# A two-layer streaming encoder on one core: the merge of its instruction strands keeps the strand chosen last until another is 0.04 of its own length behind

## The chip, the cores and the metric

The kernel runs on one core of one Trainium2 chip. The metric is the device time of one execution in microseconds (us). The kernel before was executed three times for timing and once under the profiler. The engines are named as in the profile: PE is the matrix engine (PEld its weight load), DVE the vector engine, ACT the scalar engine, POOL the general engine, SP the engine that only starts transfers.

## What is computed

The input x has 512 tokens of width 1024 in float32, and there is a memory of 256 tokens. Layer 0 mixes its tokens by a recurrence over 12 heads of 64 (with attention of 4 more heads into the memory beside it), layer 1 by chunked attention over 12 heads (with the same memory attention). Each layer ends in a gated feed-forward part with a convolution of width 3. Cut to what matters here:

```python
def wkv7_scan(r, w, k, v, a, b):                  # layer 0, one step per token
    def step(state, inp):
        r_t, w_t, k_t, v_t, a_t, b_t = inp
        sa = einsum('bhvk,bhk->bhv', state, a_t)
        state = state * w_t + sa * b_t + v_t * k_t     # outer products, 64x64 a head
        return state, einsum('bhvk,bhk->bhv', state, r_t)
...
for layer in range(2):
    h = rms_norm(x, ln1[layer])
    p = h @ w_in[layer]
    if layer == 0:
        mix = rwkv7_time_mix(h, p[..., :3 * 768], ...)   # scan, norm per head, gate g
    else:
        mix = chunk_attention(q, k_pad, v_pad, bias)     # own chunk and 8 before
    mo = memory_attention(q_mem, mem_n, w_mem_kv[layer])
    x = x + concatenate([mix, mo]) @ w_out[layer]
    x = x + conv_glu(rms_norm(x, ln2[layer]), ...)
return rms_norm(x, ln_f)
```

## The kernel before

**Data and products.** Activations lie with features on the 128 partitions and the 512 tokens along the free axis. A float32 product is made of three products of rounded halves: high by high (L221), low by high (L222) and high by low (L225). A projection to 128 features is 24 such matmuls of 128x512 over 8 slices of the width. In the text they are called wide matmuls. Their weights come by DMA into `wraw`; ACT rounds the high half `whi` (L175), and DVE (L183) or ACT (L180) makes the low half `wlo`.

**The recurrence.** Heads go in six pairs, each in three parts, which are Python generators:

- `prepare(i)` (L1085) makes r, k, v and the decay of pair i with three projections (72 wide matmuls), normalises k over each head, mixes each projection with its shifted self (the results `krv` and `v`, L1121), makes the scores within each chunk of 64 tokens (L1169), copies them (ACT, L1174) and starts a triangular solve on DVE. The normalisation takes sums over heads, for pairs 2 and 3 in a wide form (`head_wide`: Square on ACT L1061, split L238, sums on PE L1065 and L1066), else in a narrow one (`head_rsqrt`: sums on PE L1041).
- `front(i)` (L1249) makes the parts of pair i that need no solve or only its first half: L1259 with its mask on DVE (L1262), row sums L1283 and L1285, a copy `Rq` on ACT (L1266), L1317 with the copy `Y` (L1323), and L1334 with four small copies `Tt` (L1339).
- `back(i)` (L1359) finishes pair i: L1369 and L1377, L1383 with its copy `Tt` (L1387), two halves of L1393 (copies L1394, L1396), two halves of L1404 (DVE L1405, L1406), L1412, then eight chunks in a row of the state (L1426 on PE, L1427 on DVE, L1431 on PE). The result is copied to `yc` (ACT L1435), the gate's weights are rounded (`g2h`, ACT L1442), yc is squared (L1441, or L1061 where `head_wide` is used, for pairs 1 and 2), its sums over heads are taken (PE L1041, or L1065) and the gate is multiplied (PE L201 to L203).

All of these but the wide matmuls have tiles of 64 rows or fewer on PE, except the sums over heads.

**The attention of layer 1** goes over the same pairs of heads. A row block (L1745, L1746) makes scores for 128 queries; DVE adds the bias and takes the maximum (L1750), ACT takes the exponential (L1752), DVE the reciprocal of the sum (L1753) and the product with it (L1754). Three row blocks later (`LAG = 3`) PE transposes the block (L1760) and ACT copies it (L1762). The values (L1774) follow at the end of a pair.

**What sets the order.** The engines each run their instructions in the order in which the program lists them, with semaphores between engines. That order is made by `weave` (L87). It is given several generators, here called strands, each with a length. A strand issues some instructions of all engines and then yields the time that its PE work is held to cost, which is added to its `done`; it may also yield a time for which it must not be called, or a condition. Of the strands that may be called, `weave` calls the one with the smallest share of its length done:

```python
e = min(ready, key=lambda x: x[2] / x[1])     # L99: done / length
```

Behind it a scheduler of the framework moves instructions within each engine's list where their inputs come late by its own costs, with the order of the program as priority. `weave` is called four times:

- L1530: the end of `prepare(0)` with the low-rank projections and the memory's keys and values;
- L1538, once for each stage 0 to 4: `back(stage - 1)`, `front(stage)` and `prepare(stage + 1)`, with the lengths 13.7, 5.8 and 18.7 us;
- L1566: `back(4)`, then `front(5)` and `back(5)`, the memory attention, and a part of the output projection;
- L1840: the attention of layer 1 (a length of 50.2 us by the program's own costs) with the projections of its queries, keys and values and a part of the output projection (84.4 us).

The dense strands yield after every two wide matmuls (0.43 us in the program's costs), the small parts after 0.15 to 2.3 us. The feed-forward parts are not woven.

**Buffers.** The PSUM banks are 8: two for wide matmuls; in layer 0 four for small products and two for long sums, in the attention six for small products. Weights have three `whi`, three `wlo` and two `wraw`.

Of the kernel before, what the change touches and what calls it, by code (L numbers as in the profile page):

```python
# [83 lines left out]
    return c  # L84


def weave(gens, tc=None):  # L87

    live = [[g[0], float(g[1]), 0.0, 0.0, g[2] if len(g) > 2 else 0, None] for g in gens]
    now = 0.0
    while live:
        free = [e for e in live if e[5] is None or e[5]()]
        ready = [e for e in free if e[3] <= now]
        if not ready:
            now = min(e[3] for e in free)
            continue
        e = min(ready, key=lambda x: x[2] / x[1])  # L99
        e[5] = None  # L100
        try:
            with tc.high_priority(e[4]) if e[4] else ExitStack():
                y = next(e[0])
        except StopIteration:
            live.remove(e)
            continue
        if callable(y):
            e[5] = y
            continue
        cost, wait = y if isinstance(y, tuple) else (y, 0)  # L110
        now += cost
        e[2] += cost
        e[3] = now + wait
# [3 lines left out]
def trunk_kernel(ctx, tc, A, out):  # L117
# [1410 lines left out]
    for d_ in d2s:  # L1528
        nc.sync.dma_start(d_[:].rearrange("b m g u c i -> (b m g u) (c i)"), zero[:, 0:256])
    weave([(first, .981 * PREP_COST), (chain(lora_one(), mem_kv()), 16 * 648 + MEMKV_COST)])  # L1530
    act1 = hact
    pre = []
    lo_on[0] = 1
    for st_ in range(NPAIR - 1):
        gens = [(front(st_, Ts[st_], Ts[st_ + 1]), 1.069 * FRONT_COST), (prepare(st_ + 1, Ts[st_ + 1]), .971 * PREP_COST)]
        if st_ > 0:
            gens.insert(0, (back(st_ - 1, Ts[st_ - 1], dst_mix), 1.003 * BACK_COST))
        weave(gens, tc)  # L1538
# [21 lines left out]
    def ahead():  # L1560
# [3 lines left out]
    AHEAD = [0, 1, 2, 3, 4, 6, 7]  # L1564
    a_, b_ = NPAIR - 2, NPAIR - 1
    weave([(told(back(a_, Ts[a_], dst_mix), "back"), 1.5 * BACK_COST),  # L1566
           (chain(front(b_, Ts[b_]), later(6000), back(b_, Ts[b_], dst_mix, other_tiles, lambda: "back" in over)),
            1.5 * (FRONT_COST + BACK_COST)),
# [420 lines left out]
```

## Time and profile before

| | us |
|---|---|
| median of three runs | 1302.93 (1302.65 to 1303.38) |
| the profiled execution: its own time | 1301.85 |
| the profiled execution: span of the page | 1300.1 |
| PE busy in the span | 1278.6 |
| stages of the recurrence, all calls of L1538 | about 83 to 302 |
| last weave of layer 0 | about 302 to 350 |
| attention of layer 1 | about 735 to 924 |

The span runs from the first to the last instruction of the profile; 1.75 us of the profiled execution's own time lie around it. Starts in the profile are counted from the beginning of the span. In a timeline row the first number is the start, the second the duration, and a bracket at the end gives how long the engine stood idle ahead of it and what released it. In order listings a count behind a row (x8) joins neighbours of one form; a row on the 64x64 products holds two heads, so that the profile's count for the same work is twice as high.

### The profile page before, as it was taken

To read this page: it belongs to the slowest core of one execution; us is meant where nothing else is said; L and a number is where in the kernel's file an instruction comes from. 1 tells how busy PE (TensorE), PEld (TensorE's weight loads), DVE (VectorE), ACT (ScalarE), POOL (GpSimd) and SP (SyncE) were. 2 spreads that over 40 slices of the span, in tenths; PEclk is the share of its full clock that TensorE was granted. 3 is DMA by queue.
4 is the path that set the end of the run, shared out by engine and by line. 5 is a ranking of instruction groups with operands and counts; after the bars stand their busy time and mean duration, and the time that the engine had idled before them with its cause. 6 is when DMAs were issued, how large, how long until landed. Compare 5 with 4: busy or idle time off the path is not lost.

```text
span 1300.1 us, 26329 instructions
## 1 busy us (share of the span) xinstructions
PE 1278.6 (98%) x10420; PEld 1100.9 (85%) x10420; DVE 1041.8 (80%) x1956; ACT 836.5 (64%) x1380; POOL 137.6 (11%) x164
## 2 busy tenths in 40 slices
PE   9999999999999999999999999999999999999997
PEld 7887777777789999999888878787799999998886
DVE  7967767775589999999876876658889999998684
ACT  6666767756566666767554676657757666665562
POOL 1000000000001112110220000000011122111200
PEclk9999999999999999999999999999999999999999
DMA  6365434452236777886984332223437878879951
GB/s 202 110 177 116 112 69 106 95 113 69 82 114 148 182 175 193 189 183 176 270 179 122 123 90 85 81 95 115 130 80 183 183 173 197 186 159 285 214 141 65
DMA packets 92988, 187.42 MB, mean 144 GB/s; under 512 B 21824, under 2 KB 30144, under 8 KB 92864
## 3 DMA queue, kind: packets, MB, share of 16 engines
q1 hardware_dynamic: 68592, 129.14, 31.1%
q0 software_dynamic: 24272, 56.59, 25.0%
q8 instruction: 82, 1.34, 0.4%
q14 instruction: 42, 0.34, 0.1%
HBM read 169.48 MB, written 6.29 MB: 135 GB/s over the span
## 4 chain that ended last, share of the span: by engine, by line
PE 83%; DVE 7%; ACT 6%; issue 1%; DMA 1%; SPq 0%; ACTq 0%; DVEq 0%
PE psf L414 21%; PE psf L416 11%; PE psf L658 7%; PE psd L225 6%; PE psd L221 6%; PE psd L222 5%; PE psf L663 4%; PE psd L658 3%; PE psd L663 2%; PE pss L1774 1%; PE pss L658 1%; DVE wlo L183 1%; PE pss L1404 1%; PE pss L350 1%; PE pss L1760 1%
## 5 line engine op out<-in xcount | busy, mean ns | idle before, releaser
L468 ACT CAST whi<-raw 128x1024 fp32r<-128x1024 f32 (+1 forms) x168 | 151.8, 941 | 66.2 <-PE psf L414 37.4
L414 PE MATMUL psf<-tl,whi 128*128 128x256 f32 x672 | 168.6, 283 | 0.0
L414 PE MATMUL psf<-th,whi 128*128 128x256 f32 x672 | 168.3, 283 | 0.0
L473 DVE TENSOR_TENSOR wlo<-raw,whi 128x1024 fp32r<-128x1024 f32 (+1 forms) x126 | 131.5, 1043 | 14.3 <-ACT whi L468 14.2
L175 ACT CAST whi<-wraw 128x1024 fp32r<-128x1024 f32 x84 | 87.7, 1047 | 69.3 <-PE psd L222 36.1
L414 PEld LDWEIGHTS psf<-tl,whi 128*128 128x128 f32 x672 | 128.7, 192 | 0.0
L414 PEld LDWEIGHTS psf<-th,whi 128*128 128x128 f32 x672 | 128.5, 192 | 0.0
L221 PE MATMUL psd<-r1h,whi 128*128 128x512 f32 x264 | 108.2, 410 | 0.0
L222 PE MATMUL psd<-r1l,whi 128*128 128x512 f32 x264 | 105.6, 401 | 0.0
L183 DVE TENSOR_TENSOR wlo<-wraw,whi 128x1024 fp32r<-128x1024 f32 x65 | 79.3, 1219 | 15.9 <-ACT whi L175 13.6
L648 ACT CAST whi<-raw 128x1024 fp32r<-128x1024 f32 (+1 forms) x52 | 49.6, 954 | 65.2 <-PE psf L658 35.4
L649 DVE TENSOR_TENSOR wlo<-raw,whi 128x1024 fp32r<-128x1024 f32 (+1 forms) x52 | 56.7, 1099 | 42.6 <-ACT whi L648 33.6
L416 PE MATMUL psf<-th,wlo 128*128 128x256 f32 x504 | 81.2, 283 | 0.0
L225 PE MATMUL psd<-r1h,wlo 128*128 128x512 f32 x264 | 74.9, 405 | 0.0
L416 PEld LDWEIGHTS psf<-th,wlo 128*128 128x128 f32 x504 | 69.7, 192 | 0.0
L451 POOL DMA_DIRECT2D wlv<-in_ffn_in_dram x40 | 61.2, 1530 | 59.7 <-DVE tmp L535 58.7
L494 ACT ACTIVATE tmp<-tmp,vec 128x512 f32<-128x512 f32 x44 | 35.9, 817 | 47.3 <-DVE tmp L481 47.1
L414 PE MATMUL psf<-r2h,whi 128*128 128x256 f32 x252 | 63.3, 283 | 0.5 <-ACT whi L468 0.5
L414 PE MATMUL psf<-r2l,whi 128*128 128x256 f32 x252 | 63.2, 283 | 0.0
L414 PE MATMUL psf<-r1h,whi 128*128 128x256 f32 x252 | 62.5, 281 | 0.5 <-ACT whi L468 0.5
L414 PE MATMUL psf<-r1l,whi 128*128 128x256 f32 x252 | 62.1, 279 | 0.0
L221 PEld LDWEIGHTS psd<-r1h,whi 128*128 128x128 f32 x264 | 49.5, 188 | 13.0 <-issue 2.5
(608 smaller groups left out, 3545.7 us busy)
## 6 DMA issues: line engine op xcount, KB each, us to landing
raw<-in_ffn_in_dram SPq DMA_DIRECT2D x42, 512.0 KB, 3.8
raw<-in_ffn_in_dram SPq DMA_DIRECT2D x84, 256.0 KB, 4.2
wlv<-in_ffn_in_dram POOLq DMA_DIRECT2D x40, 512.0 KB, 8.0
raw<-in_ffn_out_dram SPq DMA_DIRECT2D x30, 512.0 KB, 5.9
raw<-in_ffn_out_dram POOLq DMA_DIRECT2D x24, 512.0 KB, 8.0
wraw<-in_wA_dram SPq DMA_DIRECT2D x20, 512.0 KB, 4.2
wraw<-in_w_out_dram SPq DMA_DIRECT2D x16, 512.0 KB, 3.9
wraw<-in_ffn_outp_dram SPq DMA_DIRECT2D x16, 512.0 KB, 4.7
```

The lines of the kernel that those rows point to most:

```text
L175: high = lambda: pin(SC.copy(hi[:, :n], raw))
L183: pin(V.tensor_tensor(lo[:, :n], raw, hi[:, :n], op=ALU.subtract))
L221: PE.matmul(ps, wh[:, j * P:(j + 1) * P], ah, start=start and n == 0, stop=False)
L222: dense_at[0] = PE.matmul(ps, wh[:, j * P:(j + 1) * P], al, start=False, stop=False)
L225: dense_at[0] = PE.matmul(ps, wl[:, j * P:(j + 1) * P], act(k)[0], start=False, stop=stop and n == len(ks) - 1)
L414: PE.matmul(ps, wh[:, o + k * P:o + k * P + P], x[k][n], start=k == n == 0, stop=False)
L416: PE.matmul(ps, wl[:, ol + k * P:ol + k * P + P], x[k][0], start=False, stop=k == 3)
L451: GP.dma_start(self.low[:].rearrange("p (a s) -> p a s", a=2), self.second, accum_op=ALU.add)
L468: keep(SC.copy(hi[:, :n], self.pair(what) if n > S else self.raw[:, what]))
L473: keep(V.tensor_tensor(lo[:, :n], self.pair(what) if n > S else self.raw[:, what], hi[:, :n], op=ALU.subtract))
L658: PE.matmul(ps[:], a[:, k0 + i, ts], hi[:, i * S:i * S + S], start=bool(first) and (first is True or t in first) and a is act[0] and i == ...
L663: PE.matmul(ps[:], act[0][:, k0 + i, ts], lo[:, i * S:i * S + S], start=False, stop=bool(last) and t in last and i == n - 1)
```

## The change

`weave` remembers which strand it called last and takes 0.04 off that strand's share. The same strand is called again, as long as it may be called, until another one's share is more than 0.04 below its own. After a turn passes, the other strand has the same allowance, so that two strands can be up to 0.04 apart in either direction. Nothing else is changed: the instructions, tiles, buffers and strands are the same, and lines below L87 move down by four (L1404 becomes L1408).

```diff
+WEAVE_STAY = 0.04
+
+
 def weave(gens, tc=None):
...
-    now = 0.0
+    now, last = 0.0, None
     while live:
         free = [e for e in live if e[5] is None or e[5]()]
         ready = [e for e in free if e[3] <= now]
         if not ready:
             now = min(e[3] for e in free)
             continue
-        e = min(ready, key=lambda x: x[2] / x[1])
+        e = min(ready, key=lambda x: x[2] / x[1] - (WEAVE_STAY if x is last else 0))
+        last = e
```

By the program's costs 0.04 is 0.55 us for `back`, 0.23 us for `front`, 0.75 us for `prepare`, 2.0 us for the attention strand and 3.4 us for the projections beside it.

What moves is seen in the order on each engine. Three places stand for it.

**PE in stage 1, where `back(0)` goes through L1393 (now L1397).** L221, L222 and L225 (now L225, L226 and L229) are the wide matmuls of `prepare(2)`. Before:

```order
L221 MATMUL psd<-r1h,whi 128x512
L222 MATMUL psd<-r1l,whi 128x512
L1393 MATMUL pss<-VT,Tt_94 64x128 x8
L221 MATMUL psd<-r1h,whi 128x512
L222 MATMUL psd<-r1l,whi 128x512
L225 MATMUL psd<-r1h,wlo 128x512 x4
L1393 MATMUL pss<-VT,Tt_94 64x128 x8
L225 MATMUL psd<-r1h,wlo 128x512 x4
```

Now:

```order
L225 MATMUL psd<-r1h,whi 128x512
L226 MATMUL psd<-r1l,whi 128x512
L225 MATMUL psd<-r1h,whi 128x512
L226 MATMUL psd<-r1l,whi 128x512
L1397 MATMUL pss<-VT,Tt_94 64x128 x16
L229 MATMUL psd<-r1h,wlo 128x512 x8
```

The two halves of L1393 stand together, and four wide matmuls instead of two are ahead of the first. The halves of L1404 (now L1408) have joined in the same way in the stages where they stood apart. Over the list of PE for the recurrence, the places where wide matmuls are followed by products of 64 rows or fewer go from 73 to 64, and the returns from 75 to 68.

**PE and ACT at the end of stage 2, from the scores of `prepare(3)` on.** Here `back(1)` is in its chain of states, `front(2)` comes to L1334, and `prepare(3)` has given its scores (L1169) and goes on with the projection whose v is still to come. PE before:

```order
L225 MATMUL psd<-r1h,wlo 128x512 x6
L1169 MATMUL pss<-KB,AR 64x64 x16
L1317 MATMUL pss<-Tc,Lc 32x16 x32
L1431 MATMUL psl<-MQ,W 64x64 x2
L225 MATMUL psd<-r1h,wlo 128x512 x2
L221 MATMUL psd<-r1h,whi 128x512
L222 MATMUL psd<-r1l,whi 128x512
L221 MATMUL psd<-r1h,whi 128x512
L1334 MATMUL pss<-Y,Tn 16x16 x32
```

Now:

```order
L1173 MATMUL pss<-KB,AR 64x64 x16
L1321 MATMUL pss<-Tc,Lc 32x16 x32
L229 MATMUL psd<-r1h,wlo 128x512 x2
L1430 MATMUL psl<-W,MQ 64x64 x2
L1435 MATMUL psl<-MQ,W 64x64 x2
L229 MATMUL psd<-r1h,wlo 128x512 x2
L1338 MATMUL pss<-Y,Tn 16x16 x24
L1430 MATMUL psl<-W,MQ 64x64 x2
L1435 MATMUL psl<-MQ,W 64x64 x2
L1338 MATMUL pss<-Y,Tn 16x16 x8
L229 MATMUL psd<-r1h,wlo 128x512
```

Behind the scores the chain of states had only its last product (L1431) left, and now has three steps and the last product (L1435). From L1169 to the gate's product L201 there were 13 wide matmuls and there are 14; between the gate's products and the sums L1065 there were 8 and there are 4. ACT before:

```order
L1339 COPY Tt_94<-pss 16x8x16
L1435 COPY tmp<-psl 128x512
L1442 CAST g2h<-tmp 128x128
L1339 COPY Tt_94<-pss 16x8x16 x3
L1061 ACTIVATE tmp<-tmp 128x512
L180 ACTIVATE wlo<-wraw 128x1024
L238 CAST tmp<-tmp 128x512
L1266 COPY Rq<-AR 128x512
```

Now:

```order
L1343 COPY Tt_94<-pss 16x8x16 x4
L1270 COPY Rq<-AR 128x512
L1439 COPY tmp<-psl 128x512
L1446 CAST g2h<-tmp 128x128
L1065 ACTIVATE tmp<-tmp 128x512
L1125 ACTIVATE v<-tmp,om 128x512
L242 CAST tmp<-tmp 128x512
L184 ACTIVATE wlo<-wraw 128x1024
```

The copy `Rq` and all four copies `Tt` now stand ahead of yc (L1439) and g2h; v stands between the Square and the split that the sums read, and the rounding of `wlo` has gone behind. In stages 1 and 3 the same moves are found; in stage 3 there stand `whi` (L179), `Rq` and `wlo` (L184) ahead of yc, which stood behind the Square, so that ACT runs three more operations ahead of yc there.

**PE in the attention of layer 1, near its beginning.** L1745 and L1746 are scores, L1760 transposes, L221 to L225 wide matmuls of a projection. Before:

```order
L222 MATMUL psd<-r2l,whi 128x512
L221 MATMUL psd<-r2h,whi 128x512
L1760 MATMUL pss<-cst,sb 128x128
L1745 MATMUL pss<-ks,qs 128x384
L1746 MATMUL pss<-kl,qs 128x384
L222 MATMUL psd<-r2l,whi 128x512
L1760 MATMUL pss<-cst,sb 128x128
L1745 MATMUL pss<-ks,qs 128x384
L1746 MATMUL pss<-kl,qs 128x384
L225 MATMUL psd<-r2h,wlo 128x512 x4
L1760 MATMUL pss<-cst,sb 128x128 x2
```

Now:

```order
L229 MATMUL psd<-r2h,wlo 128x512 x8
L1749 MATMUL pss<-ks,qs 128x384
L1750 MATMUL pss<-kl,qs 128x384
L1764 MATMUL pss<-cst,sb 128x128 x2
L1749 MATMUL pss<-ks,qs 128x512
L1750 MATMUL pss<-kl,qs 128x512
L1764 MATMUL pss<-cst,sb 128x128 x2
L1749 MATMUL pss<-ks,qs 128x512
L1750 MATMUL pss<-kl,qs 128x512
L1764 MATMUL pss<-cst,sb 128x128 x3
```

Scores and transposes of several row blocks stand behind each other with no wide matmul between. Over the whole attention the number of blocks of attention work with wide matmuls on both sides goes from 85 to 49.

## The prediction

> **What bounds the kernel now.** I read the page's busy line and its chain of waits first, then the windows by stage, then the waits of PE, and last the timelines of the places that move.
>
> ```profile
> span 1300.1 us, 26329 instructions
> PE 1278.6 (98%) x10420; PEld 1100.9 (85%) x10420; DVE 1041.8 (80%) x1956; ACT 836.5 (64%) x1380; POOL 137.6 (11%) x164
> PE 83%; DVE 7%; ACT 6%; issue 1%; DMA 1%; SPq 0%; ACTq 0%; DVEq 0%
> ```
>
> PE is busy for 1278.6 of 1300.1 us and holds 83% of the chain that ends last. So the change can win only what PE stands idle (21.5 us in all) or what its matmuls lose at switches between shapes, and it can lose wherever it makes PE wait. The windows tell where the idle time lies; the columns are window, length, then busy time of PE, PEld, DVE, ACT and POOL with their counts, the clock, the DMA share and GB/s.
>
> ```profile
> 28.00:83.00 55.00, 53.88 (x366) 46.65 (x367) 49.94 (x114) 30.63 (x52) 0.31 (x1) 1.00 0.41 115
> 83.00:302.00 219.00, 213.28 (x3219) 161.58 (x3217) 151.65 (x431) 151.20 (x291) 14.77 (x17) 1.00 0.48 109
> 302.00:350.00 48.00, 47.80 (x669) 35.38 (x669) 31.62 (x94) 27.64 (x76) 0.00 (x0) 1.00 0.09 28
> 735.00:924.00 189.00, 185.04 (x1062) 145.90 (x1061) 128.50 (x337) 126.81 (x293) 2.13 (x12) 1.00 0.31 101
> ```
>
> In the four woven parts PE is idle for 1.12, 5.72, 0.20 and 3.96 us, together 11.0 us. This is the most that better cover could give. The feed-forward parts keep their order and cost nothing. DVE and ACT are at 69% in the stages and at 68% and 67% in the attention: on average there is slack, and only the order within a few microseconds can make PE wait. The waits that the change touches:
>
> ```profile
> PE pss L1377 <- DVE ML L1262: 0.7, 1, 0.7
> PE pss L1760 <- DVE st L1753: 1.1, 2, 0.7
> PE pss L1774 <- ACT ptT L1762: 1.0, 3, 0.4
> ```
>
> **Switches between shapes.** No instruction is added or removed, so the sum is one of switches and waits. The price of a switch is seen where L1404 cuts into wide matmuls:
>
> ```profile
> 125.18 0.50 PE L221 MATMUL psd<-r1h,whi 128*128 128x512 f32 x1
> 125.52 0.40 PE L222 MATMUL psd<-r1l,whi 128*128 128x512 f32 x1
> 125.84 1.09 PE L1404 MATMUL pss<-ML,W 64*64 64x128 f32 x16
> 126.86 0.50 PE L221 MATMUL psd<-r1h,whi 128*128 128x512 f32 x1
> 127.20 0.39 PE L222 MATMUL psd<-r1l,whi 128*128 128x512 f32 x1
> 127.43 0.40 PE L221 MATMUL psd<-r1h,whi 128*128 128x512 f32 x1
> ```
>
> From L222 to the next L221 the distance is 0.23 us (127.20 to 127.43), the pitch of a wide matmul in a row. From L222 into L1404 it is 0.32 (125.52 to 125.84), 0.09 more; the first wide matmul behind small ones takes 0.34 (126.86 to 127.20), 0.11 more. In the recurrence 9 entries and 7 returns fall away: 9 x 0.09 + 7 x 0.11 = 1.6 us. In the attention the entries into 64-row products and the returns from them go up by three each, and six returns from transposes fall away; at a similar tenth each, this cancels. I take **-1.6**, with ends at -1.7 and 0, the latter where PE would wait for an input anyway.
>
> The Trainium skill bears on this in TensorEngine Tiling (Array Packing), section Key Properties: a change of the tiling mode, and not of the tile alone, drains the matrix engine. The 0.09 and 0.11 us agree with a drain; it gives no price, and by that rule alone the change would end at -1.6, which is the side of the first rival.
>
> **Stage 1, L1393 and the two waits behind it.** Before, PE stood idle ahead of L1393:
>
> ```profile
> 117.55 0.74 ACT L1387 COPY Tt<-pss 32x256 f32<-32x256 f32 x2
> 118.05 1.44 PE L1393 MATMUL pss<-VT,Tt 64*64 64x128 f32 x16 [0.64 <-ACT Tt L1387]
> ```
>
> Two more wide matmuls now stand ahead of it. They take 2 x 0.23 us out of this 0.64: **-0.46**. The copy L1387 comes no earlier, so that 0.18 stays, and the two matmuls aren't missed later, since L1393 in one piece needs no cover between its halves. L1377's wait of 0.7 has about one wide matmul more ahead: -0.2. Against it stands the sum over heads of `back(0)`:
>
> ```profile
> 144.48 1.15 PE L1169 MATMUL pss<-KB,AR 64*64 64x64 f32 x32
> 151.99 1.05 PE L1041 MATMUL pss<-cst,tmp 128*128 128x2 f32 x8 [0.58 <-ACT tmp L1441]
> ```
>
> PE waits 0.58 us for the Square. By the new order ACT does `Rq`, all four copies `Tt` and a `wlo` ahead of it. I add up both engines from L1169: the Square is done at about 9.8 us, PE arrives at about 9.0, so that the wait grows from 0.58 to 0.8: +0.2. L1377 and L1041 together: **0**.
>
> **Stage 2, the gate and the norm of `back(1)`.** Here ACT's order matters most:
>
> ```profile
> 193.65 0.25 ACT L1339 COPY Tt<-pss 16x128 f32<-16x128 f32 x1
> 193.80 0.57 ACT L1435 COPY tmp<-psl 128x512 f32<-128x512 f32 x1
> 194.28 0.29 ACT L1442 CAST g2h<-tmp 128x128 fp32r<-128x128 f32 x1
> 194.59 0.82 ACT L1339 COPY Tt<-pss 16x128 f32<-16x128 f32 x3
> 195.44 0.63 ACT L1061 ACTIVATE tmp<-tmp 128x512 f32<-128x512 f32 x1
> 195.98 1.04 ACT L180 ACTIVATE wlo<-wraw 128x1024 fp32r<-128x1024 f32 x1
> 196.93 0.60 ACT L238 CAST tmp<-tmp 128x512 fp32r<-128x512 f32 x1
> 197.44 0.62 ACT L1266 COPY Rq<-AR 128x512 f32<-128x512 f32 x1
> ```
>
> ```profile
> 187.86 1.15 PE L1169 MATMUL pss<-KB,AR 64*64 64x64 f32 x32
> 194.62 0.50 PE L201 MATMUL psl<-gsh,g2h 128*128 128x512 f32 x1 [0.31 <-ACT g2h L1442]
> 197.58 0.50 PE L1065 MATMUL pss<-tmp,blk 128*128 128x512 f32 x1
> ```
>
> L201 stands 6.76 us behind L1169 and waited 0.31 us of it for g2h. Now g2h is later by `Rq` (0.62) and the three copies (0.82): 1.4 us. PE is later too: one wide matmul (0.23), 12 more products of the state (L1169's 32 take 1.15, so 0.43 us) and some three more pairs of switches (0.6) make 1.3 us. The wait at L201 stays near 0.3. Behind it PE has four wide matmuls instead of eight (0.9 us for 1.9) to the sums L1065, while ACT has Square, v and split to do, where v is the same work as `krv`:
>
> ```profile
> L1121 ACT ACTIVATE v<-tmp,om x5: 704/721/727, 110.3 to 279.7; 128x512 f32<-128x512 f32 x5
> ```
>
> From g2h on that is 0.6 + 0.7 + 0.6 = 1.9 us, against three gate matmuls and four wide ones on PE (7 x 0.23 = 1.6). So L1065 waits about 0.3: **+0.3** (0 to 0.5). What covered the split before, the four wide matmuls, now runs ahead of L201.
>
> **Stage 3** has the same place with more ahead of yc:
>
> ```profile
> 226.93 1.15 PE L1169 MATMUL pss<-KB,AR 64*64 64x64 f32 x32
> 234.03 0.30 ACT L1442 CAST g2h<-tmp 128x128 fp32r<-128x128 f32 x1
> ```
>
> g2h was ready 7.4 us behind L1169's start. It now comes behind one more copy `Tt` (0.26) and `whi`, `Rq` and `wlo` (1.0 + 0.6 + 1.0 by the forms above): 10.3. PE comes to L201 at 10.0 by its new list: scores and L1317 1.7, 20 wide matmuls 4.7, state products 1.75, L1334 0.7, switches 1.2. The wait is 0.3 to 0.5, and the split behind it costs again 0.3: **+0.7** (0 to 0.9).
>
> **Behind these places.** In stages 2 and 3 PE reaches the next scores about 0.6 us earlier relative to L1066, while the chain of ten microseconds on DVE that feeds them is as long as it was: +0.2 each, **+0.4** (0 to 0.8). In the last weave the sum L1041 of `back(4)` stands 2.1 instead of 3.1 us behind the last product of the state, and yc, Square and their hops need about 2.4: **+0.3** (0 to 0.5).
>
> **The attention.** With 0.04 in both directions a turn moves 2 x 2.0 us of attention work against 2 x 3.4 us of projections. A row block of 512 keys costs:
>
> ```profile
> L1750 DVE CUSTOM_DVE_ANT_0 sb<-pss,big 128x512 f32<-128x512 f32 x12 | 8.1, 683 | 0.3 <-PE pss L1746 0.2
> L1752 ACT ACTIVATE sb<-sb,st 128x512 f32<-128x512 f32 x12 | 8.7, 722 | 0.4 <-DVE st L1753 0.3
> L1752 ACT ACTIVATION_READ_ACCUMULATOR sb<-sb,st 128x1 f32 x48 | 9.0, 187 | 0.0
> L1753 DVE RECIPROCAL st<-st 128x1 f32<-128x1 f32 x48 | 7.5, 160 | 4.6 <-ACT sb L1752 4.0
> L1754 DVE TENSOR_SCALAR sb<-sb,st 128x512 f32<-128x512 f32 x12 | 5.8, 482 | 0.1
> L1762 ACT COPY ptT<-pss 128x512 f32<-128x512 f32 x12 | 6.8, 582 | 1.2 <-PE pss L1760 1.2
> ```
>
> From its scores to its transposes a block needs 0.68 + 0.72 + 0.19 + 0.16 + 0.48 = 2.2 us and the hops. ACT is held 0.72 + 0.19 + 0.58 = 1.49 us by each, DVE 1.33. On PE scores, transposes and the block's part of the values take about 1.3, so a burst of attention alone makes ACT the slowest engine by 0.15 to 0.2 us per block, and the roundings of weights that the next wide matmuls need queue there too. Three blocks of lag give 3.9 us on PE alone, which still covers 2.2 us and hops, but not with a rounding of 1.0 us in front twice. The lower bound is 0, or even the 2 us of L1760's and L1774's waits; the upper bound is a wait of 0.3 to 0.5 at each of some ten bursts, 4 us. The existing waits are 0.3 to 0.7 each, and I take three more of that size: **+1.5**.
>
> The Trainium skill says in TensorE: Matmul & The Clock Gate, section Step-by-step: what each phase is for, that only weight loads are pulled ahead while the matmuls stay in program order. The brackets of the rows for L201 and L1393 agree: wide matmuls that were free to run stood behind them. By that rule a wait at the head of a burst is paid in full, which is the side of the second and third rival.
>
> **Sum.** -1.6 - 0.46 + 0 + 0.3 + 0.7 + 0.4 + 0.3 + 1.5 = +1.1 us. From the profiled execution's 1301.85 us, which is 1.08 under the median of 1302.93, that is 1303.0 for an execution like it and **1304.1** for a median: no change that can be told, since a difference under 0.2% (2.6 us) can't be told from none here.
>
> **Rivals.**
>
> 1. *The merges pay and the waits shrink.* ACT has slack at 69%, and the longer wide runs ahead of the bursts let roundings finish early. For it: 1.6 us of switches are sure to go, and the largest single waits (0.64, 0.7) get cover. Against it: the copies ahead of g2h. It gives -1.6 - 0.46 - 2.0 (the attention's waits) = -4: 1299.
> 2. *Slower: the bursts of attention run into ACT.* The place is L1760 and L1774, the price 0.5 us at each of 8 to 10 bursts; it decides once a rounding stands ahead of an exponential in most bursts. For it: 1.49 us on ACT against 1.3 on PE per block, and halved alternations. Against it: the lag of three, and only 1.1 + 1.0 us of such waits now. It gives +4 to +6: 1308.
> 3. *Slower: the stages wait at the norm.* If the copies ahead of g2h delay the sums L1041 and L1065 in each of four stages by 0.8 to 1.2 us rather than 0.3 to 0.7, that is +3.5 to +4 with the switches taken off: 1306.5. For it: the queue ahead of yc in stage 3. Against it: PE is late there too.
> 4. *The scheduler takes the turns apart again.* The order shows that it doesn't: 73 entries became 64 and 85 blocks 49. What remains of this is inside the forecast.
>
> **How the numbers follow.** Forecast within 2.6 us of the median before, with its own range 1300.3 to 1305.5: 0.39. First rival 0.23, second 0.24, third 0.14. The two slower rivals have 0.38 together: slower 0.38, same 0.39, faster 0.23. The range goes from the first rival's centre to past the second's: 1299.0 to 1309.0.
>
> **What would show it.** Right: PE's idle time in 83 to 302 within 1 us of 5.72, its wait at L1397 near 0.2, new waits of about 0.3 at the new L1069 and 0.8 at the new L1045, and two to four more waits at the new L1764 or L1778, so that PE's idle time in the attention is near 5.5. Wrong: an idle time in the attention of 8 us or more (second rival) or under 3 (first), more than 8 in the stages (third), or a change outside the woven parts.

## The result and the profile after

The changed kernel takes 1309.26 us (median of six runs, 1307.38 to 1313.0), the kernel before 1303.16 beside it: 6.1 us slower, ratio 1.0052 with a 95% interval of 1.0041 to 1.0062. The profiled execution took 1308.06 us, 6.2 more than that of before. The page after, with its span, busy line and chain of waits:

```profile
span 1306.3 us, 26326 instructions
PE 1282.4 (98%) x10420; PEld 1105.8 (85%) x10420; DVE 1042.3 (80%) x1956; ACT 835.8 (64%) x1380; POOL 137.2 (11%) x164
PE 85%; DVE 5%; ACT 5%; DMA 2%; issue 2%; SPq 0%; ACTq 0%; DVEq 0%
```

PE is idle for 23.9 us instead of 21.5, and busy for 3.8 us more with the same instructions. Where it happens is seen at the first matmuls of one form of the feed-forward parts, which have no weave; the row of the same work before stands first, then that of after (first and last start at its end):

```profile
L414 PE MATMUL psf<-th,whi x672: 277/283/367, 391.3 to 1162.2; 128*128 128x256 f32 x168
```

```profile
L418 PE MATMUL psf<-th,whi x672: 277/283/367, 396.1 to 1168.3; 128*128 128x256 f32 x168
```

The recurrence ends 4.8 us later. By the end of the second feed-forward part it is 6.1. Between them lies the attention, 0.8 us longer: the windows from the first matmul of its value projection (745.4 and 750.6) to the next feed-forward part are, before and after,

```profile
745.40:953.00 207.60, 203.64 (x1140) 161.29 (x1139) 147.29 (x357) 141.11 (x311) 3.44 (x11) 1.00 0.30 95
```

```profile
750.60:959.00 208.40, 205.26 (x1139) 162.36 (x1137) 146.21 (x357) 139.85 (x311) 3.15 (x11) 1.00 0.30 95
```

So most of the loss, 4.8 of 6.1 us, is in the recurrence. The same window as in the prediction, and the largest waits of PE between 83 and 350 us:

```profile
83.00:302.00 219.00, 210.38 (x3164) 160.99 (x3164) 152.35 (x435) 149.38 (x283) 14.76 (x17) 0.97 0.48 106
```

```profile
PE pss L1338 <- issue: 2.9, 2, 1.7
PE pss L1321 <- DMA Tc<-d2a: 1.1, 1, 1.1
PE pss L1338 <- ACT Y L1327: 0.8, 4, 0.2
PE pss L1045 <- ACT tmp L1154: 0.8, 1, 0.8
PE pss L1287 <- DVE ML L1266: 0.7, 2, 0.4
PE pss L1069 <- ACT tmp L242: 0.7, 1, 0.7
PE pss L1381 <- DVE ML L1266: 0.4, 1, 0.4
```

Two things are new. The granted clock, the third number from the right in the window, is 0.97 where it was 1.00. And PE waited twice within L1338, 2.9 us in all, for "issue", which is a wait that nothing shown in the profile ends. The places, in timelines of stages 0, 3 and 4:

```profile
105.39 0.95 PE L1321 MATMUL pss<-Tc,Lc 32*32 32x16 f32 x60 [1.14 <-DMA Tc<-d2a]
...
229.38 0.33 PE L1338 MATMUL pss<-Y,Tn 16*16 16x16 f32 x24 [0.21 <-ACT Y L1327]
230.90 0.33 PE L1338 MATMUL pss<-Y,Tn 16*16 16x16 f32 x24 [1.20 <-issue]
...
273.19 0.32 PE L1338 MATMUL pss<-Y,Tn 16*16 16x16 f32 x22 [0.17 <-ACT Y L1327]
275.23 0.25 PE L1338 MATMUL pss<-Y,Tn 16*16 16x16 f32 x10 [1.71 <-issue]
```

In stages 3 and 4 PE stops in the middle of 64 equal matmuls whose inputs are all there; in stage 0 it waits for a transfer, Tc. The clock record has three stretches at half clock, of 3.41, 6.83 and 3.41 us, and each begins 1.1 to 1.9 us behind the end of one of these three stops. The windows cut at the bounds of the record (the clock is the third number from the right):

```profile
103.09:106.51 3.42, 2.23 (x97) 1.94 (x96) 2.25 (x5) 2.96 (x7) 0.00 (x0) 1.00 0.90 254
106.51:109.92 3.41, 3.41 (x71) 2.33 (x71) 1.51 (x3) 2.41 (x7) 0.00 (x0) 0.50 0.15 17
...
229.39:232.80 3.41, 2.21 (x82) 1.67 (x83) 0.74 (x4) 2.82 (x8) 0.00 (x0) 1.00 0.16 17
232.80:236.21 3.41, 3.41 (x21) 1.86 (x21) 1.99 (x6) 1.82 (x3) 0.00 (x0) 0.50 0.11 18
236.21:239.63 3.42, 3.42 (x11) 2.26 (x11) 0.98 (x2) 2.67 (x5) 0.86 (x1) 0.50 0.34 53
...
273.76:277.17 3.41, 1.94 (x58) 1.32 (x59) 0.28 (x1) 2.43 (x7) 0.00 (x0) 1.00 0.49 72
277.17:280.59 3.42, 3.42 (x21) 1.96 (x17) 1.94 (x5) 1.21 (x4) 0.00 (x0) 0.50 0.12 36
```

In the windows of 3.41 us ahead of the half clock PE was busy for 2.23, 2.21 and 1.94 us. The four windows at half clock are 13.7 us, in which PE does at most half of its work: up to 6.8 us are lost, as much as the whole difference. A higher busy time of PE in a window of lower clock is no more work, only slower work. The six runs agree: the mean clock and the time go together, from 0.994 and 1307.4 us to 0.990 and 1313.0 us, 1.4 us for each 0.001, where 0.001 of 1306 us is 1.3 (one run of 0.994 took 1310.4). Of 83 runs of the kernel before that stand beside the experiments one has 0.997 and the others 0.998 or 0.999; the end of the program alone, where PE has no work left, holds the mean under 1.

### The profile page after: what moved, and what is told of

It is laid out like the page before. It is cut to its first block, busy times and chain, and to the rows that moved or that the text cites. A ratio compares the mean times of both kernels' runs of the same rounds, so it can differ in the third digit from the quotient of the medians.

```text
span 1306.3 us, 26326 instructions
## 1 busy us (share of the span) xinstructions
PE 1282.4 (98%) x10420; PEld 1105.8 (85%) x10420; DVE 1042.3 (80%) x1956; ACT 835.8 (64%) x1380; POOL 137.2 (11%) x164
## 4 chain that ended last, share of the span: by engine, by line
PE 85%; DVE 5%; ACT 5%; DMA 2%; issue 2%; SPq 0%; ACTq 0%; DVEq 0%
PE psf L418 21%; PE psf L420 10%; PE psf L662 7%; PE psd L229 6%; PE psd L225 6%; PE psd L226 6%; PE psf L667 4%; PE psd L662 3%; PE psd L667 2%; PE pss L1778 1%; PE pss L662 1%; PE pss L1408 1%; PE pss L1764 1%; PE pss L354 1%; PE pss L1397 1%
## 5 line engine op out<-in xcount | busy, mean ns | idle before, releaser
L179 ACT CAST whi<-wraw 128x1024 fp32r<-128x1024 f32 x84 | 87.9, 1049 | 69.4 <-PE psd L226 29.8
L225 PE MATMUL psd<-r1h,whi 128*128 128x512 f32 x264 | 107.4, 407 | 0.0
L226 PE MATMUL psd<-r1l,whi 128*128 128x512 f32 x264 | 106.5, 403 | 0.0
L229 PE MATMUL psd<-r1h,wlo 128*128 128x512 f32 x264 | 78.0, 419 | 0.0
L225 PEld LDWEIGHTS psd<-r1h,whi 128*128 128x128 f32 x264 | 50.1, 190 | 13.1 <-issue 1.9
```

The source lines that it names most:

```text
L179: high = lambda: pin(SC.copy(hi[:, :n], raw))
L225: PE.matmul(ps, wh[:, j * P:(j + 1) * P], ah, start=start and n == 0, stop=False)
L226: dense_at[0] = PE.matmul(ps, wh[:, j * P:(j + 1) * P], al, start=False, stop=False)
L229: dense_at[0] = PE.matmul(ps, wl[:, j * P:(j + 1) * P], act(k)[0], start=False, stop=stop and n == len(ks) - 1)
```

## The experiments

Letters in the expectations: theory A is that idle time of PE among small products takes its clock to half, theory D that the stops in L1338 come from the fetch of PE's instructions; rival C is the second of the prediction's rivals. The kernel before took 1302.98, 1302.68, 1302.54 and 1302.39 us beside the four groups of runs below; each ratio is to it.

### Which weave it is

The allowance became an argument of `weave` (`stay`, 0 unless given), and was given to some calls alone:

```diff
-def weave(gens, tc=None):
+def weave(gens, tc=None, stay=0.0):
...
-        e = min(ready, key=lambda x: x[2] / x[1] - (WEAVE_STAY if x is last else 0))
+        e = min(ready, key=lambda x: x[2] / x[1] - (stay if x is last else 0))
...
-        weave(gens, tc)
+        weave(gens, tc, WEAVE_STAY)
```

The last two lines are those of stay_stages; the other kernels have the argument in the calls that they name.

> The allowance of 0.04 in the first weave alone, all other weaves as before. In the changed kernel this weave gives the scores of pair 0 3.5 us later than before, and PE stands idle for 1.1 us in stage 0 for the transfer Tc that hangs on them. Theory A (an idle time of over 1.1 us within one window of 3.4 us takes the clock of PE to half for the next window): Tc is waited for again, one window at half clock in the profile around 106 us, +1.5 to +3.5 us on the time before. Rival B (the loss comes from the bunches of small products in the stages, and the clock only goes with it): no wait over 0.3 us, the time within 0.5 us of before.

1302.33 us, ratio 0.9997 (0.9988 to 1.0006): nothing. Theory A expected a wait for Tc here, and there is none over 0.2 us: the transfers of Tc begin late as well (97.6 us, before 90.7, changed kernel 98.5), but not late enough.

> The allowance in the weaves of stages 0 to 4 alone. Theory A with starvation of PE for instructions at L1338: the idle times of 1.2 and 1.7 us in L1338 of stages 3 and 4 are there again, each with at least one window of 3.4 us at half clock behind it, no such window in stage 0, mean clock 0.994 to 0.996, +3 to +5.5 us on the time before. Rival B (waits of the gate and the norm behind a longer queue on ACT): the clock is 0.998 as before and the loss is in the waits at L1045, L1069 and L205 (over 2 us together).

1308.73 us, ratio 1.0044 (1.0027 to 1.0061), clock 0.991 to 0.992. The stages alone bring the loss, with the same two stops in L1338, 1.20 and 1.67 us, and half clock behind both, for 10.2 and 3.4 us. A wait of 1.8 us for the split at L1069 in stage 1 came up as well, of the kind that rival B meant, with no half clock behind it. There is no half clock in stage 0: the late Tc of the changed kernel needs the first weave and the stages together.

> The allowance in the last weave of layer 0 and in the attention alone. Theory A: no window at half clock, the clock 0.998, the time between -0.5 and +1.5 us of before (the changed kernel lost 0.8 us between the starts of the attention and of the feed-forward part behind it). Rival C of the prediction (bursts of attention run into ACT): +4 us or more.

1303.83 us, ratio 1.0007 (0.9997 to 1.0016). The loss of 4 us or more that bursts of attention running into ACT would bring is not there.

### Giving the fetch time

```diff
+        if i in (3, 4):
+            fb = ps_s()
+            for _ in range(8):
+                PE.matmul(fb[:], blk1[:], r1h[:, 0], start=True, stop=True)
         ps = ps_s((P, 8, 16))
```

> The changed kernel, and in the fronts of stages 3 and 4 eight matmuls of 128x512 more ahead of L1338 whose result nobody reads: 2 x 8 x 0.233 = 3.7 us more work for PE. Theory A with starvation for instructions: the eight give the fetch 1.9 us, the idle times of 1.2 and 1.7 us go, and so do the windows at half clock behind them (2.9 + 5.1 us): in spite of more work the time is 3 to 5 us under that of the changed kernel (1304 to 1306). Rival B (PE is bound by its work and by waits for ACT there): +3 to +4 us on the changed kernel, 1312 to 1313.

1306.85 us, ratio 1.0036 (1.0023 to 1.005), 1303.5 to 1313.5 in ten runs: 2.4 under the changed kernel in spite of 3.7 us more work, but less of a gain than expected. In the profile the stop in stage 4 is gone, that in stage 3 is 0.69 us, and no window is at half clock. Other waits came up (1.7 us at L1069, 1.3 at L1412), and single runs have a clock of 0.993. It points to theory A with D and does not settle it.

### Where the stops come from

Three kernels test theory D. The first is the kernel before with a bunch of short products:

```diff
+        if i in (1, 2, 3):
+            fb = ps_s((P, 8, 16))
+            for c in range(20):
+                for u in range(4):
+                    rw = slice(u * 32, u * 32 + 16)
+                    PE.matmul(fb[rw, c % 8], Tn[rw, c % 8, 0:16], Y[rw, c % 8], start=True, stop=True, tile_position=(u * 32, u * 32))
         ps = ps_s((P, 8, 16))
```

> The kernel before, and in the fronts of stages 1, 2 and 3 eighty more products of 16x16 ahead of L1334 whose result nobody reads. By the rows of L1334 (64 records in 0.69 us) they are 160 records and 1.7 us of work a stage, 5.2 us in all. Theory D (PE is starved of instructions: they come in blocks of 256 by transfers of 16,384 bytes, and a bunch of short products uses up a block faster than the next one comes): at least two of the three bunches show an idle time of 0.7 to 2 us in their middle with no engine named as its releaser, and windows at half clock follow some of them: +8 to +16 us. Rival E (the two idle times of the changed kernel wait for something of its new order, a copy or a transfer): no such idle time, clock 0.998, +5 to +6 us.

1323.91 us, ratio 1.0162 (1.014 to 1.0183), clock 0.990: 21 us for 5.2 us of work, more than expected. The waits of PE (L1335 are the added products, L1340 and L1437 the old L1334 and L1431):

```profile
PE pss L1340 <- issue: 3.1, 2, 2.5
PE psl L1437 <- issue: 1.7, 1, 1.7
PE pss L1335 <- issue: 1.5, 2, 1.1
```

No weave was touched here, so the stops are not of the new order as such: rival E falls. For 24 us in all the clock is at half. The other two are the changed kernel with 32 products of 16x16 added behind L1338 in one front, 64 matmuls and 64 weight loads on PE, since a plain float32 product is two of each in the profile (not two heads, as the part on the profile before has it). The diff is that of shift_blocks, and shift_early has `i == 0`:

```diff
+        if i == 2:
+            fb = ps_s((P, 8, 16))
+            for n in range(32):
+                rw = slice(n % 4 * 32, n % 4 * 32 + 16)
+                PE.matmul(fb[rw, n // 4], Tn[rw, n // 4, 0:16], Y[rw, n // 4], start=True, stop=True, tile_position=(n % 4 * 32, n % 4 * 32))
         for u in range(4):
```

> The changed kernel, and in the front of stage 2 thirty-two more products of 16x16 behind L1338 whose result nobody reads: 0.35 us of work, and 128 instructions of PE, half a block, so that all later blocks begin 128 instructions earlier in the list. Theory D: the idle times in L1338 of stages 3 and 4, which came 1279 instructions apart, five blocks of 256, move: they stand about 128 instructions earlier in the list (in L1321), and are shorter there, since wide matmuls lie in the first half of the block then. With them the half clock goes or gets less: 2 to 6 us under the changed kernel. Rival E: the idle times of 1.2 and 1.7 us stay at the same products of L1338, the time within 1 us of the changed kernel.

1306.02 us, ratio 1.0028 (1.0018 to 1.0037). The stops in L1338 of stages 3 and 4 are gone, as theory D has it. Others came up, not in L1321 as expected but in the added products (1.5 us), in L1435 (the old L1430, 0.5 us) and in L1421 of the last weave (1.4 us). Half clock is left in one place, 6.8 us from 190.3 us on; the wait for Tc in stage 0 is 1.0 us and has none behind it.

> The changed kernel, and in the front of stage 0 the thirty-two products of 16x16 behind L1338 that shift_blocks had in stage 2: the order in stages 1 to 4 is that of the changed kernel, and every block begins 128 instructions earlier in the list there. Theory D: no idle time over 0.5 us in L1338 of stages 3 and 4; the wait for Tc in stage 0 remains (1.1 us and at times its half clock). The time is 2 to 6 us under the changed kernel (1303 to 1307). Rival E: as the changed kernel, 1308 to 1310.

1302.32 us, ratio 1.0003 (0.9991 to 1.0015), 1300.65 to 1308.58 in ten runs. With 0.35 us more work, and the order of the changed kernel from stage 1 on, 6.9 us of its median are gone (6.3 against the kernel before beside each). The timeline of stage 3 and the waits of PE between 83 and 350 us (L1345 are the added products, L1435 the old L1430):

```profile
226.66 0.55 PE L1338 MATMUL pss<-Y,Tn 16*16 16x16 f32 x48 [0.20 <-ACT Y L1327]
...
227.52 0.28 PE L1338 MATMUL pss<-Y,Tn 16*16 16x16 f32 x16
```

```profile
PE pss L1421 <- issue: 1.9, 1, 1.9
PE pss L1338 <- ACT Y L1327: 1.1, 5, 0.3
PE pss L1345 <- issue: 1.1, 1, 1.1
PE pss L1386 <- DVE ML L1266: 1.0, 2, 0.6
PE psl L1435 <- issue: 0.7, 1, 0.7
```

L1338 runs through. The wait for Tc, expected to remain, has gone too, so that the 6.3 us are not of the stops alone: the wait and the half clock behind it were up to 2.8 of them. Three stops of 3.7 us are left at other places, without half clock in the profiled execution; the clock of single runs goes down to 0.994, and the slowest of them took 1308.58.

The count of PE's records in the trace (matmuls, weight loads and its semaphore instructions) ahead of each stop of over 0.45 us that no engine ends, in all runs of this study (the other kernels, that of before too, have none):

| kernel | PE goes on at, us | line | idle, us | records ahead | remainder by 256 |
|---|---|---|---|---|---|
| changed | 230.9 | L1338 | 1.20 | 5314 | 194 |
| changed | 275.2 | L1338 | 1.71 | 6593 | 193 |
| stay_stages | 231.7 | L1338 | 1.20 | 5313 | 193 |
| stay_stages | 277.2 | L1338 | 1.67 | 6594 | 194 |
| filler | 229.6 | old L1338 | 0.69 | 5314 | 194 |
| small_bunch | 199.7 | old L1334 | 2.49 | 4801 | 193 |
| small_bunch | 241.7 | added | 1.07 | 6082 | 194 |
| small_bunch | 245.2 | old L1431 | 1.73 | 6338 | 194 |
| small_bunch | 290.2 | old L1334 | 0.65 | 7618 | 194 |
| shift_blocks | 191.6 | added | 1.51 | 4289 | 193 |
| shift_blocks | 276.1 | old L1430 | 0.52 | 6849 | 193 |
| shift_blocks | 307.6 | L1421 | 1.40 | 7874 | 194 |
| shift_early | 107.9 | added | 1.07 | 1730 | 194 |
| shift_early | 270.9 | old L1430 | 0.74 | 6850 | 194 |
| shift_early | 302.9 | L1421 | 1.91 | 7873 | 193 |

All fifteen stand at one place of a grid of 256 instructions, in six kernels. The page of the kernel before has the transfers that fit it (the queue, packets, MB, share):

```profile
q8 instruction: 82, 1.34, 0.4%
```

These are 82 transfers of 16,384 bytes, one for 256 of PE's 20,979 records if each is an instruction of 64 bytes. In small_bunch, with 962 records more, there are 85. In the changed kernel one of them starts at 228.58, takes 0.90 us, and PE goes on at 230.90; the next stop's starts at 272.87, takes 0.96, and PE goes on at 275.23. From the start of the transfer to PE's next product it is 2.32 and 2.36 us. In all fifteen stops it is 2.2 to 2.9 us, while in the kernel before the least time from such a start to the same place of the next block is 4.45 us. So PE is starved of instructions where the transfer begins too late for its rate: a wide matmul of 0.23 us uses two, while L1173, L1321 and L1338 use 64, 128 and 128 in 1.1, 0.7 and 0.7 us.

### What idle time does to the clock

The diff is that of wait_only; wait_long has 15 for 7.

```diff
             SC.copy(Y[:], ps[:])
+            for _ in range(7 if i in (1, 2, 3) else 0):
+                SC.copy(Y[:], Y[:])
```

> The kernel before, and in the fronts of stages 1, 2 and 3 the copy Y (L1323) is followed by seven copies of Y onto itself, one behind the other, 1.2 to 1.9 us on ACT ahead of L1334: PE idles that much longer in each. No order of PE changes. Theory A (idle time among small products takes the clock down): at least one of the three idle times is followed by a window at half clock in a run, mean clock under 0.998, +5 to +10 us in all. Rival F (the half clock comes from the bunched order and not from the idle time): clock 0.998 to 0.999 and +3 to +5.5 us, the sum of the three waits.

1305.97 us, ratio 1.0023 (1.0013 to 1.0034), clock 0.997 to 0.999. The windows of 3.41 us with most idle time have 0.96 and 0.90 us of it, and no half clock follows. The idle times were shorter than meant, so this is no test of rival F. The order of PE did not stay either: for the longer work on ACT the scheduler moved wide matmuls ahead of the products that wait for Y.

> The kernel before, and in the fronts of stages 1, 2 and 3 fifteen copies of Y onto itself instead of the seven of wait_only, which gave 0.9 to 1.0 us more idle time in a stage: PE should idle some 2 us at L1334 of each, with the order of PE as before. Theory A: most of the three idle times are followed by a window at half clock, mean clock 0.992 to 0.996, the time 10 to 14 us over before (7 of it the three waits). Rival F (the half clock comes from the bunched order): clock 0.998 to 0.999, +6 to +8 us.

1323.86 us, ratio 1.0163 (1.0146 to 1.018), clock 0.987 to 0.988. Against the expectation, PE's order is not that of before: between L1317 and L1334 of stage 1 stand 50 wide matmuls and the gate's three products, where there were 5 wide ones. PE idles 7.5 us at L1334 (4.7 in stage 2), and half clock follows in all three stages, for 27 us in all. Two pairs of windows of its profile, the idle one and the next:

```profile
205.09:208.51 3.42, 0.00 (x0) 0.00 (x0) 0.69 (x1) 3.42 (x8) 0.00 (x0) 1.00 0.14 41
208.51:211.92 3.41, 2.31 (x68) 1.78 (x68) 2.42 (x12) 2.37 (x9) 0.86 (x1) 0.50 0.69 168
...
256.29:259.71 3.42, 1.43 (x68) 1.25 (x68) 2.45 (x13) 2.54 (x8) 0.86 (x1) 1.00 0.91 225
259.71:263.12 3.41, 3.41 (x42) 2.55 (x41) 2.17 (x9) 1.47 (x5) 0.00 (x0) 0.50 1.03 249
```

In the window from 205.09 PE runs nothing at all, so idle time by itself takes the clock down, and rival F falls as the only cause. The bunch counts too, though. Two windows ahead of half clock, of small_bunch and shift_blocks, have little idle time, and most of their matmuls are 16x16 (208 of 211 and 121 of 142):

```profile
193.74:197.15 3.41, 3.03 (x213) 2.37 (x212) 0.40 (x1) 3.26 (x8) 0.00 (x0) 1.00 0.18 19
```

```profile
186.88:190.29 3.41, 2.99 (x143) 2.05 (x143) 1.79 (x5) 3.24 (x10) 0.00 (x0) 1.00 0.18 19
```

PE is busy there for 3.03 and 2.99 us, and the stop that belongs to each (2.49 and 1.51 us) lies all or mostly behind the start of the half clock. So a bunch of small products with 0.4 us of idle time was enough in these two, and idle time is not the whole cause. In the changed kernel the stops are still needed for the half clock: shift_early has the same products in stages 3 and 4, no stop in L1338 and no half clock.

### Looking for a faster version

The first of these kernels has the allowance in two stages, the others 0.02 instead of 0.04:

```diff
-        weave(gens, tc)
+        weave(gens, tc, WEAVE_STAY if st_ in (1, 2) else 0.0)
...
-WEAVE_STAY = 0.04
+WEAVE_STAY = 0.02
```

> The allowance in the first weave and in stages 1 and 2 alone; stages 0, 3 and 4, the last weave and the attention as before. Theory A with D: no idle time over 1 us, the clock as before, and the time between -2 and +0.3 us of before, by what the merged products save. If the merges were worth nothing or the waits for the gate and the norm cost more: +0.5 us or more at a clock of 0.998.

1302.56 us, ratio 1.0001 (0.9991 to 1.001), clock 0.997 to 0.999: no gain. Three of ten runs have 0.997, and in the profiled execution half clock follows a wait of 1.3 us at L1069 in stage 1.

> The changed kernel with 0.02 for 0.04. In the front of stage 3 eight products of 16x16 instead of 24 stand ahead of the interruption by the state, the state is one step further, and prepare's wide matmuls lie as in the changed kernel. Theory D: it depends on where the blocks begin; the front of stage 3 has still 384 instructions in some 5 us, so that an idle time of up to 1.2 us can be there: +0 to +5 us on before, the clock telling which (each 0.001 of it under 0.998 is 1.3 us). A loss of over 2 us at a clock of 0.998 would speak for the waits of the norm instead.

1301.62 us, ratio 0.999 (0.998 to 0.9999), the only version under the kernel before by its interval, by 0.9 us. No stop for instructions is in its profile.

> 0.02 for 0.04, and only in the first weave and in stages 0 to 4; the last weave and the attention as in the kernel before, since the allowance there gave +0.9 us (stay_last_att). If the parts add up: the 1301.6 of stay_002 less some 0.4 us, half of that, 1301.2 to 1301.6, a ratio of 0.9985 to 0.9995. If a new idle time from the fetch of instructions comes up in the last weave, since its order against the blocks is another: 1302 to 1304 at a clock of 0.997 or less in some runs.

1302.87 us, ratio 1.0002 (0.9993 to 1.0011). The gain is not there. Either the parts do not add, or the 0.9 us of stay_002, whose interval ends at 0.9999, were little more than chance; these runs do not tell which.

## Why the prediction was wrong

The forecast was no change, 1304.1, with 0.38 for slower; the time lies just over the end of the range, 1309.0. The step that failed is the first of its sum: "No instruction is added or removed, so the sum is one of switches and waits." A term was missing, the fetch of PE's instructions with the half clock behind it: 2.9 us of stops and up to 6.8 us at half clock, the latter with the wait for Tc. I had read the clock in four windows, 1.00 in each, and taken it as given, while the trace before showed no stop of this kind.

- **The order is not slower.** This is what shift_early shows. The form of the feed-forward parts that was shown at the head starts there at 389.6 us, 1.7 before that of the kernel before, with 3.7 us of stops for instructions ahead of it:

```profile
L418 PE MATMUL psf<-th,whi x672: 274/283/365, 389.6 to 1161.8; 128*128 128x256 f32 x168
```

  In this execution the merges and the better cover are thus worth at least the 1.6 that the switches were given; by its median shift_early is level with the kernel before. How much of it is switches was not measured by itself.
- **The stops and the clock took it back.** 2.9 us of "issue", 1.1 for Tc, and up to 6.8 us at half clock. Together they are up to 10.8 us against the +4.8 of the recurrence; the difference is what the order saves, and what the half clock cost less than its bound.
- **The signs.** PE's idle time in 83 to 302 is 8.6 us, the sign given for the third rival (over 8), but it is made by the stops and Tc (4.0 us) and not by the norm. In the attention it is 3.2, neither the 5.5 of the forecast nor a rival's sign.
- **Stage 1.** L1397 (before L1393) does not wait at all, where 0.18 was forecast to stay, and L1381 0.4 us for 0.7. At the sum of `back(0)` (L1041, now L1045) 0.8 was forecast and none came. The 0.8 at L1045 in the list is that of `prepare` in stage 0, which I had not looked at.
- **Stage 2, +0.3.** It did not come, and the 0.31 at the gate's product, forecast to stay, has gone as well. The gate and the sums after, with the ACT work that each needs:

```profile
194.21 0.50 PE L205 MATMUL psl<-gsh,g2h 128*128 128x512 f32 x1
...
195.94 0.41 PE L1069 MATMUL pss<-tmp,blk 128*128 128x512 f32 x1
```

```profile
193.85 0.30 ACT L1446 CAST g2h<-tmp 128x128 fp32r<-128x128 f32 x1
...
195.20 0.61 ACT L242 CAST tmp<-tmp 128x512 fp32r<-128x512 f32 x1
```

  g2h is ready at 194.15, the split at 195.81, each about 0.1 us ahead of PE, and neither row has a wait. The chain on ACT is nearly as tight as was worked out, but PE comes just behind it.
- **Stage 3, +0.7, the scores behind it, +0.4, and the last weave, +0.3.** None of these waits came: the list of waits has neither L205 nor L1173, and L1069 only once, in stage 1. In the changed kernel PE is late in stage 3 by its own stop; but shift_early, where it isn't, has no such wait either. The queue on ACT was counted right: there g2h is ready 10.2 us behind the first score of stage 3 (10.3 forecast). PE comes to the gate at 10.8, not 10.0, so the cover was counted too small.
- **Attention, +1.5.** Measured +0.8 in the profile and +0.85 in stay_last_att, inside the bounds. The mechanism was wrong: PE's idle time fell from 3.96 to 3.14 us, and its busy time rose by 1.6. Why the same matmuls take longer there is open. The three added pairs of switches would be 0.6 of it at the price used; the prediction let them cancel against six returns from transposes, and no run measures either.
- **The rivals.** The second came near the time (1308) by a mechanism that is not there, the third (1306.5) named the right stages and the wrong wait. The first, better merges and waits, has the direction that the profile of shift_early shows ahead of the feed-forward parts, but its 4 us in all are seen in no run.

What stays open. First, why the transfers of instructions begin late in the changed kernel: that at 228.58 began when PE had started 5263 records, the same transfer of before at 223.37 with 5044 (by the count of the table). Between 225.98 and 229.39 the DMA engines were 0.85 busy with other transfers, but whether these or the bunch delayed it was not tried. Second, what exactly sets the half clock. Windows with 1.2 to 1.5 us of idle time went without it (one in stay_stages ahead of 136.17 with 1.35, one in shift_early ahead of 304.84 with 1.51, both with wide matmuls or products of 64 rows beside it), while one in stay_002 had it with 0.88 and those of small_bunch and shift_blocks with 0.4. The size of the products seems to count, but no rule was found: a window of shift_blocks ahead of 104.96, with 1.20 us idle among products of 64 and 32 rows, much like that of the changed kernel ahead of 106.51, went without it. The Trainium skill, in TensorE: Matmul & The Clock Gate, section What's actually happening, gives a free-running window of 3413 ns and a clock of one half behind at least one idle window. The stretches of 3.41 us agree with the window; that it must be idle does not hold here, since PE was busy for 57 to 65% of the three windows ahead of the half clock in the changed kernel.

## What to carry to other kernels

When instructions are only reordered, count PE's instructions per microsecond in the new order: a bunch of short products can outrun the fetch, and then the time depends on where blocks of 256 begin. A stop of 1 to 2 us on PE may cost twice, by itself and by 1.7 us for each window at half clock behind it, so read the granted clock of every run first. Before an order is judged by a time, run it once more with a few idle instructions ahead: 128 of them were worth over 6 us here, with the wait for Tc that went as well. An experiment that adds work on one engine can change the order on another, as wait_long did: read the order again before it is said to be the same.

## What was not expected of the hardware

- PE's instructions come during the run, in 82 transfers of 16,384 bytes, and PE stops where a block isn't there: fifteen stops of 0.5 to 2.5 us, all at one place of a grid of 256 instructions.
- The clock goes to half for multiples of 3.41 us, and not only behind idle windows: PE was busy for 57 to 65% of those in the changed kernel, and for 89% of one in small_bunch that was full of 16x16 products.
- One kernel can spread by 8 to 10 us from run to run (shift_early 1300.65 to 1308.58, filler 1303.50 to 1313.54), while the 83 runs of the kernel before in the four groups lie within 2.7 us (1301.66 to 1304.29).
